# One ring for weights and modulation tiles, a new plan for the modulation sums, and a first norm fed by two channel tiles at a time

## The chip, the cores and the metric

The kernel runs on one core of a Trainium2 chip. The metric is the device time of one execution in microseconds (us). Before the change it is 1752.94 us, the median of three runs (1749.55 to 1754.62). The engines are TensorE (PE, with its weight loads as PEld), VectorE (DVE), ScalarE (ACT), GpSimd (POOL) and SyncE (SP), which here issues DMAs only.

## The reference, cut to what matters

Two layers with separate weights act on 384 tokens, 128 of a prompt and 256 of a sample, each with 1024 channels. Every layer is a half-step feed-forward block, a mixer (attention, a gating unit and a Fourier mix) and a second half-step feed-forward block. What the change touches is the modulation: nine vectors of 1024 per layer and per condition (prompt, sample), from a product of the condition with an own matrix of 4 MB for each.

```
m = (silu(cond) @ W['w_mod'][l] + W['b_mod'][l]).reshape(cond.shape[0], 1, N_MOD, D_MODEL)
z = _modulate(_rmsnorm(h, W['g_norm'][l, 0]), m[:, :, 0], m[:, :, 1])      # x * (1 + scale) + shift
h = h + 0.5 * m[:, :, 2] * _swiglu(z, w_gate, w_up, w_down)                # 1024 -> 2816 -> 1024
z = _modulate(_rmsnorm(h, W['g_norm'][l, 1]), m[:, :, 3], m[:, :, 4])
...mixer; h = h + m[:, :, 5] * mixed
z = _modulate(_rmsnorm(h, W['g_norm'][l, 2]), m[:, :, 6], m[:, :, 7])
h = h + 0.5 * m[:, :, 8] * _swiglu(z, w_gate, w_up, w_down)
```

## The kernel before, in words

Activations lie transposed, 128 channels by 384 tokens (hT, eight tiles; "channel tile k" is one of them). Each large matrix comes in pieces of 512 KB (`raw`, four row blocks of 128 by 256 columns, so runs of 1 KB in memory). ACT casts a piece to its high part (`whi`, L476), DVE subtracts to get the low part (`wlo`, L483), and TensorE forms three products per block: high with high (L500), high weights with low activations (L501), low weights with high activations (L502). A piece feeds 24 products of 384 columns. The parts have NB = 6 buffers, so splits run up to six pieces ahead of TensorE.

The program is a list of units, each one piece's products. After a unit come the split of the piece six further on (`ensure`), then what stands in `later`: evacuations, and one `mods.pop`. All engines run their streams in order; the order is the order in which the code is written. The four `raw` buffers are reused in turn, and SP waits for DVE to finish the piece four before.

Of the 18 modulation vectors (called segments (layer, index) here), 16 are summed on DVE by `ModPhase`: a segment's matrix comes in eight tiles of 512 KB (`mraw`, two buffers of their own, asked for by POOL, L168). For each tile there is one multiply-accumulate for each condition (`macc`, L178 for the first tile, L181 for the others), then four folds per segment (a transpose L192 into PSUM, a sum L193). Three units after the last fold, TensorE adds four small products (`msel`, L202) and DVE writes the result (`modt`, L204). `MOD_PLAN` says which segments are summed in which feed-forward block. Each `pop` issues as many steps as make the progress even over the units of the block. The first block has (0,2) to (0,7), the second five segments, the third five, the fourth and both mixers none.

Segments (0,0) and (0,1), scale and shift of the first norm, go another way, since the first block can't start without them. SP loads them in slices of 128 columns (`rawm`, runs of 512 B), two slices (one of each segment) for each channel tile; TensorE multiplies them (`modacc`, L245), ACT copies out (`accs`, L248), TensorE selects (L252), DVE adds the bias (L253). `start_z` then makes the normalised tile: ACT scales and shifts (L380) and rounds it to the high part (L381), DVE subtracts (L383). `start_joint` runs all eight channel tiles through the first six pieces into six PSUM banks, with the modulation of tile k+1 in between.

The names to follow: `start_joint`, `start_z`, `mod_load`, `mod_cols`, `fetch`, `split_hi`, `split_lo`, `ensure`, `ModPhase`, `ffn`, `mixer`, `prologue`.

Of the kernel before, what the change touches and what calls it, by code (L numbers as in the profile page):

```python
# [10 lines left out]
F32 = mybir.dt.float32  # L11
# [17 lines left out]
MB = 2  # L29
MOD_WAIT = 3  # L30
MOD_SLACK = 4
MOD_LAG = 3
MOD_PLAN = {
    (0, 0): [(0, s) for s in (2, 3, 4, 5, 6, 7)],
    (0, 1): [(0, 8)] + [(1, s) for s in (0, 1, 2, 3)],
    (1, 0): [(1, s) for s in (4, 5, 6, 7, 8)],
    (1, 1): [],
}
HOLD = 8
RAW_STATS = (5, 8)  # L40
START_POS = (1, 0, 0, 0, 0, 0, 0)
NX = NT + 2
NZ = 448
# [4 lines left out]
def kernel(  # L48
# [14 lines left out]
    rawp = ctx.enter_context(tc.tile_pool(name="rawp", bufs=4))  # L63
# [28 lines left out]
    prow = [tmp.tile([128, 128], F32, tag="t", name=f"prow{l}") for l in range(NL)]  # L92
# [41 lines left out]

    pending = []
# [9 lines left out]
    class ModPhase:  # L145
# [3 lines left out]
        def __init__(self, segs, n_units):  # L149
            self.segs, self.n_units = segs, max(1, n_units)  # L150
            self.loads = [(l, seg, k) for l, seg in segs for k in range(8)]
            self.raws = {}
            self.n_loaded = 0
            self.steps = deque()
            for l, seg in segs:
                for k in range(8):
                    for i in range(2):
                        self.steps.append(lambda l=l, seg=seg, k=k, i=i: self.mac(l, seg, k, i))
                for c_ in range(4):
                    self.steps.append(lambda l=l, seg=seg, c_=c_: self.fold(l, seg, c_))  # L160
            self.n_steps, self.emitted, self.unit = len(self.steps), 0, 0
            self.fins = deque()

        def load(self):
            if self.n_loaded < len(self.loads):
                l, seg, k = self.loads[self.n_loaded]
                raw = self.raws[l, seg, k] = self.pool.tile([128, 1024], F32, tag="mraw", name="mraw", bufs=MB)
                POOL.dma_start(out=raw, in_=w_mod[l][k * 128:(k + 1) * 128, seg * 1024:seg * 1024 + 1024])  # L168
                self.n_loaded += 1

        def mac(self, l, seg, k, i):
            if k == 0 and i == 0:
                self.acc = self.pool.tile([128, 2, 1024], F32, tag="macc", name="macc", bufs=1)
            while self.n_loaded < MB:
                self.load()
            raw = self.raws[l, seg, k]
            if k == 0:
                DVE.tensor_scalar(out=self.acc[:, i], in0=raw, scalar1=condT[:, 0, i:i + 1], scalar2=None,  # L178
                                  op0=ALU.mult)
            else:  # L180
                DVE.scalar_tensor_tensor(out=self.acc[:, i], in0=raw, scalar=condT[:, k, i:i + 1],  # L181
                                         in1=self.acc[:, i], op0=ALU.mult, op1=ALU.add)
            if i == 1:
                del self.raws[l, seg, k]
                self.load()
# [23 lines left out]
        def pop(self):  # L209
# [4 lines left out]
            due = min(self.n_steps, -(-self.n_steps * self.unit // self.n_units))  # L214
            while self.emitted < due:
                self.steps.popleft()()
                self.emitted += 1

        def need(self, *segs):
            while not all(x in mod_done for x in segs):  # L220
                if self.fins:
                    self.fins.popleft()[1]()
                else:
                    self.steps.popleft()()
                    self.emitted += 1
# [6 lines left out]
    def mod_load(l, seg, k):  # L232
        raw = st["startpool"].tile([128, 8, 128], F32, tag="st", name="rawm")
        c0 = seg * 1024 + k * 128
        SP.dma_start(out=raw, in_=w_mod[l][:, c0:c0 + 128].rearrange("(k p) m -> p k m", p=128))
        mod_raws[l, seg, k] = raw

    def mod_cols(l, seg, m):

        acc = ps_m.tile([128, 512], F32, tag="m", name="modacc")  # L240
        raws = [mod_raws.pop((l, seg + e, m)) for e in range(2)]
        for k in range(4):
            for j in range(4):
                kk = 4 * (j % 2) + k
                PE.matmul(acc[32 * j:32 * j + 32, 0:128], lhsT=condT[:, kk, :], rhs=raws[j // 2][:, kk, :],  # L245
                          start=(k == 0), stop=(k == 3))
        accs = st["startpool"].tile([128, 128], F32, tag="accs", name="accs", bufs=1)
        ACT.copy(accs, acc[:, 0:128])  # L248

        def fin():  # L250
            ps = abank("msel")
            PE.matmul(ps[:, 0:4], lhsT=accs, rhs=sel3, start=True, stop=True)  # L252
            DVE.tensor_tensor(out=modt[l][:, seg:seg + 2, m, :], in0=ps[:, 0:4].rearrange("p (e i) -> p e i", e=2),  # L253
                              in1=pcol[l][:, seg * 8 + m:seg * 8 + m + 9:8].unsqueeze(2).to_broadcast([128, 2, 2]),
                              op=ALU.add)
# [115 lines left out]
    def start_z(k, aside=lambda: None):  # L371
# [81 lines left out]
    def fetch(n):  # L453

        while nfetch[0] < n:
            it = items[nfetch[0]]
            k, n_ = it["shape"]
            raw = rawp.tile([128, 1024], F32, tag="raw", name="raw")
# [83 lines left out]
    def ffn(l, f, n, nxt, first=False):  # L542
        S = {}

        def open_pool():
            S["es"] = ExitStack()
            S["pool"] = mods.pool = S["es"].enter_context(tc.tile_pool(name="ffn", bufs=1))

        mods = ModPhase(MOD_PLAN[l, f], 44 - (6 if first else 2 + MOD_WAIT) + 18 - MOD_SLACK)

# [825 lines left out]
```

## Time and profile before

| quantity | us |
|---|---|
| median of three runs | 1752.94 |
| the profiled execution, its own time | 1752.7 |
| its span in the trace | 1750.9 |
| PE busy (share of the span) | 1703.3 (97%) |
| PEld, DVE, ACT, POOL busy | 1651.6, 1207.1, 716.6, 107.1 |

The profiled execution lasts 1.8 us longer than its span. A busy time of TensorE also holds pipelined overlap and stretches at a lower clock, so 97% does not say that only 3% could be saved. A product of 384 columns shows some 0.34 us in the trace, while products start every 0.17 us. A share over the whole span mixes the opening, three feed-forward blocks with modulation sums, one without, and two mixers; the stages have to be read one at a time.

### The profile page before, as it was taken

To read this page: it belongs to the slowest core of one execution; us is meant where nothing else is said; L and a number is where in the kernel's file an instruction comes from. 1 tells how busy PE (TensorE), PEld (TensorE's weight loads), DVE (VectorE), ACT (ScalarE), POOL (GpSimd) and SP (SyncE) were. 2 spreads that over 40 slices of the span, in tenths; PEclk is the share of its full clock that TensorE was granted. 3 is DMA by queue.
4 is the path that set the end of the run, shared out by engine and by line. 5 is a ranking of instruction groups with operands and counts; after the bars stand their busy time and mean duration, and the time that the engine had idled before them with its cause. 6 is when DMAs were issued, how large, how long until landed. Compare 5 with 4: busy or idle time off the path is not lost.

```text
span 1750.9 us, 25549 instructions
## 1 busy us (share of the span) xinstructions
PE 1703.3 (97%) x10081; PEld 1651.6 (94%) x10081; DVE 1207.1 (69%) x1789; ACT 716.6 (41%) x1217; POOL 107.1 (6%) x177
## 2 busy tenths in 40 slices
PE   7899998899999999999999999999999999999997
PEld 6899998888999999999999999998899999999997
DVE  4699999674564779898969899867456467534332
ACT  4423322363553463333345333236354446433331
POOL 0011110020000000000000000002000000000000
PEclk9999999999999999999999999999999999999999
DMA  9777666453333437776647677645433342544331
GB/s 289 234 217 216 216 202 205 143 168 117 109 97 109 133 123 238 218 225 207 187 151 218 213 230 221 202 143 171 117 112 97 109 126 84 164 122 132 118 124 37
DMA packets 236340, 286.36 MB, mean 164 GB/s; under 512 B 9725, under 2 KB 212974, under 8 KB 236220
## 3 DMA queue, kind: packets, MB, share of 16 engines
q1 hardware_dynamic: 215516, 211.03, 39.5%
q0 software_dynamic: 20704, 73.70, 13.9%
q8 instruction: 79, 1.29, 0.3%
q14 instruction: 41, 0.34, 0.1%
HBM read 282.07 MB, written 2.62 MB: 163 GB/s over the span
## 4 chain that ended last, share of the span: by engine, by line
PE 83%; issue 7%; DVE 4%; DMA 4%; SPq 1%; POOL 1%; ACT 0%; POOLq 0%; DVEq 0%; ACTq 0%
PE mm L500 24%; PE mm L502 23%; PE mm L501 23%; DMA mraw<-in_w_mod_dram 2%; DVE macc L181 2%; PE mm L507 1%; PE mm L509 1%; PE mm L508 1%; DMA rawm<-in_w_mod_dram 1%; DVE wlo L483 1%; PE mm L533 1%; PE mm L534 1%; PE mm L536 1%; PE raw L502 1%; PE raw L500 1%
## 5 line engine op out<-in xcount | busy, mean ns | idle before, releaser
L483 DVE TENSOR_TENSOR wlo<-raw,whi 128x1024 fp32r<-128x1024 f32 (+1 forms) x388 | 463.4, 1200 | 371.4 <-ACT whi L476 370.7
L476 ACT CAST whi<-raw 128x1024 fp32r<-128x1024 f32 (+1 forms) x388 | 397.2, 1031 | 558.7 <-PE mm L501 461.4
L500 PE MATMUL mm<-zh,whi 128*128 128x384 f32 x1784 | 608.5, 341 | 6.6 <-DVE hu L565 4.5
L502 PE MATMUL mm<-zh,wlo 128*128 128x384 f32 x1784 | 598.8, 336 | 0.4 <-DVE wlo L483 0.4
L501 PE MATMUL mm<-zl,whi 128*128 128x384 f32 x1784 | 598.5, 335 | 0.0
L500 PEld LDWEIGHTS mm<-zh,whi 128*128 128x128 f32 x1784 | 336.4, 189 | 14.5 <-DVE hu L565 5.6
L501 PEld LDWEIGHTS mm<-zl,whi 128*128 128x128 f32 x1784 | 336.6, 189 | 2.9 <-issue 1.7
L502 PEld LDWEIGHTS mm<-zh,wlo 128*128 128x128 f32 x1784 | 336.3, 189 | 0.7 <-DVE wlo L483 0.7
L181 DVE SCALAR_TENSOR_TENSOR macc<-mraw,condT,macc 128x1024 f32<-128x1024 f32 x224 | 280.6, 1281 | 39.8 <-DMA mraw<-in_w_mod_dram 39.7
L168 POOL DMA_DIRECT2D mraw<-in_w_mod_dram x128 | 68.7, 537 | 675.1 <-DVE macc L181 385.3
L560 ACT ACTIVATE ga<-mm 128x384 f32<-128x384 f32 x80 | 38.0, 489 | 78.0 <-PE mm L502 77.8
L404 DVE SCALAR_TENSOR_TENSOR h<-mm,gq,h 128x128 f32<-128x128 f32 x96 | 34.3, 411 | 39.5 <-PE mm L502 39.2
L565 DVE TENSOR_TENSOR hu<-ga,mm 128x384 f32<-128x384 f32 x88 | 45.5, 549 | 15.4 <-PE mm L502 14.0
L285 POOL TENSOR_TENSOR rstd<-var,mhalf 128x3 f32<-128x3 f32 x6 | 9.7, 1624 | 714.3 <-DVE var L283 714.3
L269 ACT ACTIVATE sq<-h 128x384 f32<-128x384 f32 x42 | 21.9, 522 | 71.2 <-DVE h L404 71.2
L192 DVE STREAM_TRANSPOSE mT<-macc 128x512 f32<-128x512 f32 x64 | 46.3, 723 | 0.8
L193 DVE TENSOR_REDUCE msum<-mT 128x16 f32<-128x512 f32 x64 | 44.3, 692 | 2.2
L1138 ACT ACTIVATE gth<-mm,hbg 128x384 f32<-128x384 f32 x48 | 27.2, 581 | 40.2 <-PE mm L502 40.2
L501 PE MATMUL mm<-tb,whi 128*128 128x384 f32 x128 | 43.0, 336 | 0.0
L507 PE MATMUL mm<-whi,zh 128*128 128x512 f32 x96 | 39.5, 411 | 0.0
L509 PE MATMUL mm<-whi,zl 128*128 128x512 f32 x96 | 37.5, 390 | 0.0
L508 PE MATMUL mm<-wlo,zh 128*128 128x512 f32 x96 | 37.4, 390 | 0.0
(469 smaller groups left out, 2662.8 us busy)
## 6 DMA issues: line engine op xcount, KB each, us to landing
mraw<-in_w_mod_dram POOLq DMA_DIRECT2D x128, 512.0 KB, 4.5
raw<-in_ffn_w_gate_dram SPq DMA_DIRECT2D x88, 512.0 KB, 4.5
raw<-in_ffn_w_up_dram SPq DMA_DIRECT2D x88, 512.0 KB, 4.4
raw<-in_w_in_dram SPq DMA_DIRECT2D x84, 512.0 KB, 3.8
raw<-in_ffn_w_down_dram SPq DMA_DIRECT2D x80, 512.0 KB, 3.7
rawm<-in_w_mod_dram SPq DMA_DIRECT2D x16, 512.0 KB, 7.3
raw<-in_w_out_dram SPq DMA_DIRECT2D x16, 512.0 KB, 3.4
raw<-in_ffn_w_down_dram SPq DMA_DIRECT2D x16, 256.0 KB, 3.1
```

The costliest lines, as they stand in the source:

```text
L168: POOL.dma_start(out=raw, in_=w_mod[l][k * 128:(k + 1) * 128, seg * 1024:seg * 1024 + 1024])
L181: DVE.scalar_tensor_tensor(out=self.acc[:, i], in0=raw, scalar=condT[:, k, i:i + 1], in1=self.acc[:, i], op0=ALU.mult, op1=ALU.add)
L192: DVE.transpose(out=ps, in_=self.acc[:, c_ // 2, (c_ % 2) * 512:(c_ % 2) * 512 + 512])
L476: ACT.copy(it["hi"], it["raw"])
L483: DVE.tensor_tensor(out=it["w"][1], in0=it["raw"], in1=it["hi"].bitcast(F32), op=ALU.subtract)
L500: PE.matmul(ps, lhsT=wh, rhs=xh, start=first, stop=False)
L501: PE.matmul(ps, lhsT=wh, rhs=xl, start=False, stop=False)
L502: PE.matmul(ps, lhsT=wl, rhs=xh, start=False, stop=last)
L507: PE.matmul(ps, lhsT=xh, rhs=wh, start=first, stop=False)
L508: PE.matmul(ps, lhsT=xh, rhs=wl, start=False, stop=False)
L509: PE.matmul(ps, lhsT=xl, rhs=wh, start=False, stop=last)
L565: DVE.tensor_tensor(out=u, in0=S.pop(("a", m)), in1=ps[:, 0:NT], op=ALU.mult)
```

## The change

- **One ring.** Weight pieces and modulation tiles share one ring of raw buffers (`raw_tile`): four anywhere, six inside a feed-forward block. A modulation tile is asked for by SP at its place in the program, no longer by POOL with two buffers of its own.
- **One plan.** A step is now a whole tile (two accumulates) or a fold. Steps are dealt out by the time that a table gives as free on DVE in each kind of unit (`DVE_FREE`), with a target at the gate (where the block's own gate is needed). The first block loses segment (0,7) to the mixer of layer 0; the second has four segments, the third five, the fourth one.
- **The opening.** `rawm` slices are 256 columns wide, for two channel tiles at a time (four pairs of slices, p = 0 to 3, in place of eight). Their order among the weights changes. The second parameter rows and two constants are loaded by POOL in the prologue, no longer by SP. Two groups of six products of the identity with itself stand on TensorE ahead of the first product. `start_z` makes the high part straight from the scale and shift on ACT, and DVE makes the full value itself.

```
-    (0, 0): [(0, s) for s in (2, 3, 4, 5, 6, 7)],
...
+    (0, 0): ([(0, 2), (0, 3), (0, 4)], [(0, 5), (0, 6)]),
+    (0, "m"): ([], [(0, 7)]),
+    (0, 1): ([(0, 8), (1, 0), (1, 1)], [(1, 2)]),
+    (1, 0): ([(1, 3), (1, 4)], [(1, 5), (1, 6), (1, 7)]),
+    (1, "m"): ([], []),
+    (1, 1): ([(1, 8)], []),
+DVE_FREE = {"half": 27, "up": 5, "mix": 10, "att": 3, "down": 27, "resid": 0}
...
+    def raw_tile():
+        n, more = raws["n"], raws["more"]
+        if n > 3 and not more:
+            n = 0
+        raws["n"] = n + 1 if n < (5 if more else 3) else 0
+        if n < 4:
+            return rawp.tile([128, 1024], F32, tag=f"raw{n}", name="raw")
+        return more.tile([128, 1024], F32, tag=f"raw{n}", name="raw")
...
+        def mac(self, l, seg, k):
+            if k == 0:
                 self.acc = self.pool.tile([128, 2, 1024], F32, tag="macc", name="macc", bufs=1)
...
+            raw = raw_tile()
+            SP.dma_start(out=raw, in_=w_mod[l][k * 128:(k + 1) * 128, seg * 1024:seg * 1024 + 1024])
+            for i in range(2):
+                if k == 0:
...
-            due = min(self.n_steps, -(-self.n_steps * self.unit // self.n_units))
-            while self.emitted < due:
-                self.steps.popleft()()
-                self.emitted += 1
+            u, g = self.unit, self.gate_at
+            all_, before, after = 20 * len(self.segs), sum(self.free[:g]), max(1, sum(self.free[g:]))
+            at_gate = max(20 * self.n_soon, all_ * before / (before + after))
+            if u <= g:
+                due = at_gate * sum(self.free[:u]) / before
+            else:
+                due = at_gate + (all_ - at_gate) * sum(self.free[g:u]) / after
+            while self.steps and self.emitted + self.weight[0] <= due + 1e-6:
+                self.step()
...
-        raw = st["startpool"].tile([128, 8, 128], F32, tag="st", name="rawm")
...
+        raw = st["startpool"].tile([128, 8, 256], F32, tag="st", name="rawm")
+        c0 = seg * 1024 + p * 256
+        SP.dma_start(out=raw, in_=w_mod[l][:, c0:c0 + 256].rearrange("(k p) m -> p k m", p=128))
...
-            ACT.activation(out=u[:, a:b], in_=t[:, a:b], func=AF.Identity, scale=s[:, i:i + 1], bias=sh[:, i:i + 1])
-        ACT.copy(hi[:, 0:NT], u)
-        aside()
+            ACT.activation(out=hi[:, a:b], in_=t[:, a:b], func=AF.Identity, scale=s[:, i:i + 1], bias=sh[:, i:i + 1])
+        for (a, b, i) in RG:
+            DVE.tensor_scalar(out=u[:, a:b], in0=t[:, a:b], scalar1=s[:, i:i + 1], scalar2=sh[:, i:i + 1],
+                              op0=ALU.mult, op1=ALU.add)
...
+                        PE.matmul(pss[5][:, 0:128], lhsT=ident, rhs=ident, start=True, stop=True)
...
+                busy(START_BUSY[0])
+                split_hi(ids[0])
+                split_lo(ids[0])
                 fin[0] = mod_cols(l, 3 * n, 0)
-                split_hi(ids[0])
+                split_hi(ids[1])
                 fin[0]()
-                start_z(0, lambda: split_lo(ids[0]))
...
+                busy(START_BUSY[1])
+                start_z(0)
+                split_lo(ids[1])
...
+                        if (k, it) in START_MOD:
+                            p = START_MOD[k, it]
+                            fin[p] = mod_cols(l, 3 * n, p)
...
-                            prow_load(1, SP)
...
+        prow_load(1, POOL)
```

The order of the instructions shows what moved. First ACT's stream in the opening, from the last copy of the input (`h`) on: `rbs` is the row of norm factors, `accs` the modulation result, `whi` a weight piece's high part, `zh` the first product's activations. Before:

```order
L1276 COPY h_116<-xT 128x384
L322 COPY rbs<-rb 128x384
L248 COPY accs<-modacc 128x128
L476 CAST whi<-raw 128x1024
L380 ACTIVATE zu<-zt,modt_100 128x128
L380 ACTIVATE zu<-zt,modt_100 128x256
L381 CAST zh_263<-zu 128x384
```

The same place on ACT of the changed program:

```order
L1316 COPY h_116<-xT 128x384
L341 COPY rbs<-rb 128x384
L496 CAST whi<-raw 128x1024
L264 COPY accs<-modacc 128x256
L496 CAST whi<-raw 128x1024
L399 ACTIVATE zh_280<-zt,modt_100 128x128
L399 ACTIVATE zh_280<-zt,modt_100 128x256
```

Two casts of weight pieces now stand ahead of the first `zh`, one of them ahead of `accs`, and the rounding behind it is gone. Next SP's stream of DMAs behind the input's; `rawm` are the first norm's weights, `raw` weight pieces, `prow` the second layer's parameter rows, with two constants behind them before the next piece. Before:

```order
L235 DMA rawm<-in_w_mod_dram 128x8x128 x2
L461 DMA raw<-in_ffn_w_gate_dram 128x4x256
L235 DMA rawm<-in_w_mod_dram 128x8x128 x2
L461 DMA raw<-in_ffn_w_up_dram 128x4x256
L461 DMA raw<-in_ffn_w_gate_dram 128x4x256
L235 DMA rawm<-in_w_mod_dram 128x8x128 x4
L461 DMA raw<-in_ffn_w_gate_dram 128x4x256
L235 DMA rawm<-in_w_mod_dram 128x8x128 x2
L461 DMA raw<-in_ffn_w_up_dram 128x4x256
L461 DMA raw<-in_ffn_w_gate_dram 128x4x256
L235 DMA rawm<-in_w_mod_dram 128x8x128 x6
L106 DMA prow_95<-in_b_mod_dram 72x128
```

SP in the changed program, from the same place on:

```order
L251 DMA rawm<-in_w_mod_dram 128x8x256 x2
L481 DMA raw<-in_ffn_w_gate_dram 128x4x256
L481 DMA raw<-in_ffn_w_up_dram 128x4x256
L481 DMA raw<-in_ffn_w_gate_dram 128x4x256
L251 DMA rawm<-in_w_mod_dram 128x8x256 x4
L481 DMA raw<-in_ffn_w_gate_dram 128x4x256
L481 DMA raw<-in_ffn_w_up_dram 128x4x256
L481 DMA raw<-in_ffn_w_gate_dram 128x4x256
L251 DMA rawm<-in_w_mod_dram 128x8x256 x2
L481 DMA raw<-in_ffn_w_up_dram 128x4x256 x2
```

The pieces follow the last `rawm` at once, and each slice is twice as large. Last, DVE in the first feed-forward block around a segment's folds, between two evacuations of the up product (`hu`); `macc` is the modulation sum, `mT` and `msum` the fold. Before:

```order
L483 TENSOR_TENSOR wlo_1383<-raw_1379,whi_1381 128x1024
L181 SCALAR_TENSOR_TENSOR macc_1101<-mraw_1312,condT_99,macc_1101 128x1024
L192 STREAM_TRANSPOSE mT_1389<-macc_1101 128x512
L193 TENSOR_REDUCE msum_1388<-mT_1389 128x16
L483 TENSOR_TENSOR wlo_1422<-raw_1418,whi_1420 128x1024
L192 STREAM_TRANSPOSE mT_1424<-macc_1101 128x512
L193 TENSOR_REDUCE msum_1388<-mT_1424 128x16
L192 STREAM_TRANSPOSE mT_1427<-macc_1101 128x512
L193 TENSOR_REDUCE msum_1388<-mT_1427 128x16
L192 STREAM_TRANSPOSE mT_1430<-macc_1101 128x512
L193 TENSOR_REDUCE msum_1388<-mT_1430 128x16
L565 TENSOR_TENSOR hu_1457<-ga_1375,mm_1392 128x384
```

The second segment's folds in the changed program:

```order
L195 SCALAR_TENSOR_TENSOR macc_1157<-raw_1546,condT_99,macc_1157 128x1024 x2
L203 STREAM_TRANSPOSE mT_1551<-macc_1157 128x512
L204 TENSOR_REDUCE msum_1550<-mT_1551 128x16
L503 TENSOR_TENSOR wlo_1586<-raw_1582,whi_1584 128x1024
L203 STREAM_TRANSPOSE mT_1588<-macc_1157 128x512
L204 TENSOR_REDUCE msum_1550<-mT_1588 128x16
L203 STREAM_TRANSPOSE mT_1591<-macc_1157 128x512
L204 TENSOR_REDUCE msum_1550<-mT_1591 128x16
L503 TENSOR_TENSOR wlo_1624<-raw_1620,whi_1622 128x1024
L203 STREAM_TRANSPOSE mT_1626<-macc_1157 128x512
L204 TENSOR_REDUCE msum_1550<-mT_1626 128x16
L192 TENSOR_SCALAR macc_1629<-raw_1630,condT_99 128x1024 x2
```

Before, three folds stand between the last weight piece and the evacuation that TensorE's bank waits for; now one fold stands there, with the next segment's first two accumulates, and no more than two folds follow one another.

## Rows read from the trace of the kernel before

**Rows 1.** The page's first line

```profile
span 1750.9 us, 25549 instructions
```

**Rows 2.** Stages by window: first feed-forward block, mixer's start, third block

```profile
core 0: us, PE busy (x) PEld busy (x) DVE busy (x) ACT busy (x) POOL busy (x), PEclk, DMA share, GB/s
65.40:344.00 278.60, 260.02 (x1492) 257.00 (x1491) 245.12 (x297) 87.53 (x130) 24.74 (x46) 0.97 0.66 205
344.00:462.00 118.00, 117.55 (x635) 104.92 (x634) 73.50 (x151) 60.83 (x119) 14.48 (x18) 1.00 0.46 135
906.00:1184.00 278.00, 277.56 (x1630) 275.55 (x1630) 241.95 (x314) 108.38 (x167) 24.76 (x43) 1.00 0.65 201
```

**Rows 3.** What TensorE waited for, 75 to 350 us: total, times, longest

```profile
PE msel L202 <- DVE msum L193: 8.7, 3, 5.0
PE msel L202 <- DVE gq L707: 5.3, 1, 5.3
PE mm L500 <- DVE hu L565: 4.5, 3, 2.6
```

**Rows 4.** VectorE by line, 65.4 to 344 us: busy, mean ns | idle before

```profile
L181 DVE SCALAR_TENSOR_TENSOR macc<-mraw,condT,macc 128x1024 f32<-128x1024 f32 x84 | 105.0, 1281 | 17.5 <-DMA mraw<-in_w_mod_dram 17.4
...
L192 DVE STREAM_TRANSPOSE mT<-macc 128x512 f32<-128x512 f32 x24 | 17.4, 723 | 0.3
L193 DVE TENSOR_REDUCE msum<-mT 128x16 f32<-128x512 f32 x24 | 16.6, 692 | 0.8
...
L178 DVE TENSOR_SCALAR macc<-mraw,condT 128x1024 f32<-128x1024 f32 x12 | 8.6, 747 | 0.0
```

**Rows 5.** A window behind one of these waits

```profile
150.00:155.00 5.00, 2.68 (x17) 2.57 (x18) 4.93 (x9) 2.44 (x5) 0.00 (x0) 0.81 0.29 97
```

**Rows 6.** TensorE's timeline: first product of the block, first behind it

```profile
65.44 0.33 PE L500 MATMUL mm<-zh,whi 128*128 128x384 f32 x1
...
343.98 0.34 PE L500 MATMUL raw<-xh,whi 128*128 128x386 f32 x1
```

**Rows 7.** The chain of waits: third block's norm and the next norm

```profile
906.42 1.81 POOL rstd L285
1185.45 1.83 POOL rstd L285
```

**Rows 8.** The opening by window

```profile
2.00:8.00 6.00, 2.38 (x11) 2.30 (x12) 0.42 (x3) 2.06 (x5) 1.56 (x4) 1.00 0.85 286
17.00:20.00 3.00, 3.00 (x26) 2.34 (x29) 0.11 (x1) 0.85 (x1) 0.00 (x0) 0.50 1.11 343
20.00:25.00 5.00, 3.64 (x34) 2.48 (x26) 3.49 (x5) 2.62 (x6) 0.00 (x0) 1.00 1.21 293
50.00:53.00 3.00, 0.05 (x1) 0.05 (x1) 0.23 (x1) 1.21 (x2) 0.00 (x0) 0.62 1.09 371
```

**Rows 9.** The chain of waits in the opening, 42 to 52 us

```profile
42.36 1.71 SPq L106
...
47.34 4.32 DMA raw<-in_ffn_w_up_dram
```

**Rows 10.** The opening's timeline, TensorE and ACT: start, duration, idle before

```profile
15.00 0.98 ACT L380 ACTIVATE zu<-zt,modt 128x128 f32<-128x128 f32 x2
16.57 0.68 PE L500 MATMUL mm<-zh,whi 128*128 128x384 f32 x1 [2.07 <-ACT zh L381]
25.38 1.08 PE L245 MATMUL modacc<-rawm,condT 128*32 128x128 f32 x32 [0.72 <-DMA rawm<-in_w_mod_dram]
52.95 0.59 PE L252 MATMUL msel<-sel,accs 128*128 128x4 f32 x2 [5.30 <-ACT accs L248]
```

**Rows 11.** The page's costliest groups: splits of weight pieces

```profile
L483 DVE TENSOR_TENSOR wlo<-raw,whi 128x1024 fp32r<-128x1024 f32 (+1 forms) x388 | 463.4, 1200 | 371.4 <-ACT whi L476 370.7
L476 ACT CAST whi<-raw 128x1024 fp32r<-128x1024 f32 (+1 forms) x388 | 397.2, 1031 | 558.7 <-PE mm L501 461.4
```

**Rows 12.** Tile mraw: asked for to landed

```profile
DMA to landing us min/median/max: 3.7/4.5/6.8
```

More of the change, by code (lines that the diff above doesn't have):

```diff
@@ L91 @@
     mhalf = const.tile([128, 4], F32, name="mhalf")
-    prow = [tmp.tile([128, 128], F32, tag="t", name=f"prow{l}") for l in range(NL)]
+    prow = [tmp.tile([128, 128], F32, tag="t", name="prow0"),
+            tmp.tile([128, 128], F32, tag="ws", name="prow1", bufs=1)]
     pcol = [const.tile([128, 128], F32, name=f"pcol{l}") for l in range(NL)]
@@ L145, with __init__ @@
     class ModPhase:
[L149 to L153, printed above, removed]
+        def __init__(self, soon, late):
+            self.segs, self.n_soon, self.free, self.gate_at = soon + late, len(soon), [], 0
+            segs = self.segs
             self.steps = deque()
@@ L156, in __init__ @@
                 for k in range(8):
-                    for i in range(2):
-                        self.steps.append(lambda l=l, seg=seg, k=k, i=i: self.mac(l, seg, k, i))
+                    self.steps.append(lambda l=l, seg=seg, k=k: self.mac(l, seg, k))
                 for c_ in range(4):
                     self.steps.append(lambda l=l, seg=seg, c_=c_: self.fold(l, seg, c_))
-            self.n_steps, self.emitted, self.unit = len(self.steps), 0, 0
+            self.weight = deque(([2] * 8 + [1] * 4) * len(segs))
@@ L162, in __init__ @@
+            self.emitted, self.unit = 0, 0
             self.fins = deque()
[L164 to L172, printed above, removed]
-                self.acc = self.pool.tile([128, 2, 1024], F32, tag="macc", name="macc", bufs=1)
[L174 to L185, printed above, removed]
@@ L223, in need @@
                 else:
-                    self.steps.popleft()()
-                    self.emitted += 1
+                    self.step()
         def close(self):
@@ L457, in fetch @@
             k, n_ = it["shape"]
-            raw = rawp.tile([128, 1024], F32, tag="raw", name="raw")
+            raw = raw_tile()
             v = it["raw"] = raw[:, 0:k * n_].rearrange("p (k n) -> p k n", k=k)
@@ L546, in open_pool @@
             S["es"] = ExitStack()
-            S["pool"] = mods.pool = S["es"].enter_context(tc.tile_pool(name="ffn", bufs=1))
-        mods = ModPhase(MOD_PLAN[l, f], 44 - (6 if first else 2 + MOD_WAIT) + 18 - MOD_SLACK)
+            S["pool"] = mods.pool = raws["more"] = S["es"].enter_context(tc.tile_pool(name="ffn", bufs=1))
+        mods = ModPhase(*MOD_PLAN[l, f])
         def pop():
@@ L593, in run, with busy @@
+                def busy(n):
+                    for _ in range(n):
+                        PE.matmul(pss[5][:, 0:128], lhsT=ident, rhs=ident, start=True, stop=True)
                 fin = {}
-                fetch(1)
+                fetch(3)
                 loads(1)
-                fetch(3)
-                loads(2, 3)
+                loads(2)
                 fetch(4)
-                loads(4)
                 start_t(0)
+                start_t(1)
+                busy(START_BUSY[0])
+                split_hi(ids[0])
@@ L685, in ffn @@
             fill = first or i >= ids[n_first] + MOD_WAIT
+            if fill:
+                mods.free.append(DVE_FREE["up" if ty == "u" and kh == 1 else "half"])
             add_unit(piece(i, kh, (ty, mp), evs_(ev_g if ty == "g" else ev_u, mp), fill), [i])
@@ L698, in run @@
                         resid(2 * mp + e, ps, S["gate"], nxt)
-                if mp < 3:
+                if mp * 6 + kb < 24 - MOD_SLACK:
                     pop()
+            if mp * 6 + kb < 24 - MOD_SLACK and not (mp == 3 and nxt is None):
+                mods.free.append(DVE_FREE["resid" if kb == 5 else "down"])
             return run
@@ L738, in end @@
             mods.close()
+            raws["more"] = None
             S["es"].close()
@@ L1258, in prologue @@
         prow_load(0, POOL)
+        prow_load(1, POOL)
+        for dst, src in ((win, k_win), (rev, k_rev)):
+            POOL.dma_start(out=dst, in_=src)
         cond_setup()
```

138 lines of the change are left out of this document (74 added, 64 removed).

## The prediction

> **What bounds the kernel now.** The span is 1750.9 us [rows 1]. I first cut it into stages by window, since a mean over the span hides where TensorE stands still. In the third feed-forward block, 906 to 1184 us, TensorE is busy 277.56 of 278.00 us: it is the bound, and nothing on another engine can give time there. VectorE is busy 241.95 us of it, 87%, and that with five segments of modulation sums [rows 2]. The mixer's start is as full. The first feed-forward block is different: 260.02 of 278.60 us, at a mean granted clock of 0.97, with VectorE at 245.12 us. Then I read what TensorE waited for in that block: 8.7 and 5.3 us for fold results at `msel` and 4.5 us for `hu`, in sum 18.5 us, all of them VectorE [rows 3]. Each is VectorE late with its queue, since it works its stream in order. Behind such a wait the granted clock is 0.81 over five us [rows 5], so a wait costs more than its own length. By line, the six segments hold VectorE for 105.0 + 17.4 + 16.6 + 8.6 = 147.6 us, 24.6 each, and it stands idle another 17.4 us for their tiles [rows 4].
>
> How much this block loses is read off against the third. From one norm to the next there, 1185.45 - 906.42 = 279.0 us, lie 44 pieces of gate and up and 24 of down, four of these half size: 44 x 24 + 20 x 24 + 4 x 12 = 1584 products, 0.1762 us each with all that comes along [rows 7]. The first block, without its opening, has 38 such pieces and the same 24: 1440 products, 253.7 us. It takes 343.98 - 65.44 = 278.5 us [rows 6]. So 24.8 us are lost.
>
> The third place is the opening, up to 65.44 us. Its windows show the DMA queues full: their share stands above 1 (1.21 from 20 to 25 us, 1.09 from 50 to 53), as it counts packets that overlap [rows 8]. The rate depends on what is moved: 293 GB/s where mostly `rawm` with runs of 512 B is under way, 343 in a mixture, 371 where weight pieces with runs of 1 KB are alone. Then the chain shows SP at 42.36 us still sending parameter rows; the next weight piece is asked for at 47.34 and lands 4.32 us later [rows 9]. ACT waits for that piece with the next `accs` behind it, and TensorE stands still for 5.30 us [rows 10].
>
> **The opening, step by step.** From 2 to 8 us, 6.0 x 286 GB/s = 1.72 MB arrive, the input and the small rows [rows 8]. Up to the last `rawm` there follow 8.39 MB of `rawm`, six pieces (3.15 MB) and the 0.16 MB which POOL now asks for: 11.7 MB. With `rawm` in runs of 1 KB I take the mean of 343 and 371, 357 GB/s: 32.8 us, so the last slice lands at 40.8. The ends are 371 (39.5 us) and 293 (47.9); the value lies by the former since the weight pieces are the row nearest in run length.
>
> The Trainium skill, "DMA: Bandwidth & Descriptors", section Specifications, has 512 B as the least transfer for line rate, so by that rule runs of 1 KB bring nothing over 512 B. The rows disagree, 293 against 371. By the rule the last slice would land at 47.9, which is a rival below.
>
> TensorE's own path to the same place: the first product has moved back. On ACT two casts stand ahead of the first `zh`, one of them ahead of `accs`, and the first pair of slices is twice as large. The first piece lands behind 2.1 + 0.16 + 0.52 MB, at 8.0 + 7.8 = 15.8; its cast takes 1.03 [rows 11], `accs` some 0.4, the second cast 1.03, the scaled copy 0.98 [rows 10]: 19.3 us, where today the first product starts at 16.57. What stands behind these casts on ACT is `accs` and so `msel`, TensorE's start. The shorter chain saves the rounding, but its place was not what ended the wait. Then VectorE needs 0.56 for the low activations (an estimate, a third of a 1.20 us split and overhead) and two low parts of 1.20 [rows 11], and a third of channel tile 0 (6 products, 1.06) follows: 23.3. Four channel tiles of 18 products are 12.7 us, two `modacc` of twice 1.08 us [rows 10] 4.3: 40.3. So slices and TensorE arrive together, and I take 40.8. Behind it come the last `modacc` with 2.2 us, one selection of 0.59 [rows 10] and three channel tiles, 54 x 0.176 = 9.5: the block proper starts at 53.1, against 65.44: a gain of 12.3 us. The seventh piece follows the last slice on SP, lands some 1.5 us behind it and isn't needed until 53, so the 5.30 us wait goes and nothing late takes its place. The ends: 12.8 (TensorE's path alone) and 5.2 (293 GB/s).
>
> The twelve identity products lie in the wait ahead of the first product, today 2.07 us, now 2.7 longer. Taken at the 0.34 us of three times as many columns [rows 6] they would fill 4.1 of these 4.8 us. After its wait TensorE ran at a granted clock of 0.50 from 17 to 20 us, its lower level of 1.2 GHz [rows 8]. If the products keep 2.4 GHz, 1 to 2 us are won in channel tile 0, but the low parts of pieces two and three end that stage. I count zero.
>
> **The first block.** It loses segment (0,7). VectorE has 245.1 - 24.6 = 220.5 us of work left in 254 us, 87%: the share at which the third block shows no wait. The steps no longer come evenly: the order has one tile (2.5 us) in most units, where a unit takes 24 x 0.176 = 4.2 us and its piece 1.2, and one fold with two first accumulates, 1.4 + 1.5 us, ahead of the `hu` that had three folds ahead of it. A unit with two folds costs 1.2 + 2.8 = 4.0. So no unit exceeds 4.2 by itself, and the cushion of six split pieces stays whole. The ring removes waits for tiles as well: a tile is asked for when VectorE leaves the one six before, five tiles ahead. With 40 tiles and 62 pieces in 62 units that is 5 / 1.65 x 4.2 = 12.8 us of notice against 4.5 us to landing, 6.8 at most [rows 12]. SP's queue now holds these waits, and the pieces queued behind them are wanted in that same order. I take 253.7 and 1 us left over: 254.7, a gain of 23.8. Ends: 24.8, and 12.4 if half of the loss stays.
>
> **The other stages.** Mixer 0 gets segment (0,7): at most 73.5 + 24.6 = 98.1 us of VectorE in 118 us [rows 2], 83%. The nearest row, the third block with 87%, loses 0.44; I take 0.5 us. The far end is the first block of today, 24.8 lost in 278.6 at 88%: 10.5 us in 118. The second and third blocks lose nothing to VectorE today, so neither the ring nor one segment fewer brings anything there; the fourth gets one segment where the third carries five: nothing.
>
> **Sum.** 12.3 + 23.8 - 0.5 = 35.6 us; span 1750.9 - 35.6 = 1715.3. The profiled execution takes 1752.7 us, 1.8 more than its span and 0.2 less than the median of 1752.94. Predicted: 1717 us.
>
> **Rivals.**
> - *Bytes bound the opening.* If the rate stays at 293 GB/s, the gain is 5.2 there: 35.6 - 7.1 = 28.5, so 1724 us. For it: the queues are full throughout. Against: 371 with runs of 1 KB.
> - *VectorE's lag stays in part.* Half the loss remains in the first block, and mixer 0 pays 5 us, as the work is moved and not removed: 12.3 + 12.4 - 5 = 19.7, so 1733 us. For it: two accumulates now never part, so the queue comes in larger lumps. Against: the third block.
> - *Slower: the shared ring starves the weights.* Place: the three blocks with sums, 102, 100 and 108 tiles, 52 turns of the ring. If a landing exceeds 12.8 us, each turn is late by the excess, and the pieces stand in the same line. Six split pieces hide 25 us in each block. It outweighs the 35.6 us from (35.6 + 76) / 52 = 2.1 us of excess, a landing of 15 us; at 16 us it costs 166 - 76 = 90, so 1717 + 90 = 1807 us. Against: 4.5 us median. For it: SP's one queue now carries all.
> - *It doesn't do what it says.* The opening stays bound by bytes with its slow start, and the waits for `hu` and `msel` come back with the order: within 5 us of 1753.
>
> **Chances.** Forecast 0.72, bytes 0.13, lag 0.09, ring 0.03, no effect 0.03. A difference under 0.3%, 5.3 us, can't be told from none here. Faster 0.94, same 0.03, slower 0.03. The range: at the upper end the lag's 1733; at the lower end the terms' best, 12.8 + 24.8 = 37.6 or 1715, less the 3.4 us by which the fastest run lies under the median: 1711.
>
> **What would show it.** The block's first product near 53 us and the mixer's first near 308; the last `modacc` at 41 to 43 with DMA rates near 350 up to there; the first product near 19; no wait of TensorE for `msum`, `gq` or `hu` above 1 us; VectorE near 87% in the first block; no TensorE wait in mixer 0. A late `modacc` with rates under 300 would show the bytes; waits at `msel` the lag; ACT waiting for `raw` in the second and third blocks the ring.

## The result and the profile after

The changed kernel takes 1720.31 us, the median of four runs (1719.27 to 1721.3), and the kernel before 1752.49 beside it: a ratio of 0.9817, 95% interval 0.98 to 0.9834. Forecast were 1717, range 1711 to 1733. The time lies in the range, in part by luck: of the two large terms one was 3 us too large and the other 3 us too small, and the experiments found a cause for the second that the prediction does not name.

The profiled execution has this first line on its page; it answers to [rows 1]:

```profile
span 1717.6 us, 25319 instructions
```

The stages by window, with the columns of [rows 2]: most of the first feed-forward block, the start of mixer 0, and the third block.

```profile
56.00:308.00 252.00, 252.00 (x1486) 250.55 (x1484) 222.34 (x273) 90.87 (x131) 0.00 (x0) 1.00 0.71 213
308.00:426.00 118.00, 116.86 (x635) 103.83 (x629) 92.31 (x171) 60.41 (x119) 14.54 (x18) 1.00 0.58 175
...
871.00:1150.00 279.00, 278.79 (x1638) 276.42 (x1637) 242.91 (x315) 110.25 (x169) 2.31 (x3) 1.00 0.68 206
```

In the first block TensorE now stands still for nothing and its clock is 1.00, against 260.02 of 278.60 us and 0.97 in [rows 2]. VectorE's share of the block is 88% (222.34 of 252.00), just as it was before (245.12 of 278.60). Mixer 0 has taken over sums of the segment that left (92.31 us of VectorE against 73.50) and TensorE loses 1.14 us there, where it lost 0.45.

What TensorE waited for over the whole program: total, times, longest. The three rows of [rows 3] are gone, none of them has a successor.

```profile
PE modacc L261 <- DMA rawm<-in_w_mod_dram: 2.5, 2, 1.6
PE rb L338 <- POOL rstd L304: 2.2, 4, 0.9
...
PE mm L520 <- ACT A L892: 0.7, 1, 0.7
```

VectorE's accumulates on the page, busy and mean ns, then idle before them: the 17.4 us that they waited for tiles in the first block [rows 4] are 0.0 over all blocks.

```profile
L195 DVE SCALAR_TENSOR_TENSOR macc<-raw,condT,macc 128x1024 f32<-128x1024 f32 x224 | 277.2, 1280 | 0.0
```

TensorE's timeline, start and duration: the block's first product and the first one of the mixer behind it, as in [rows 6].

```profile
56.36 0.33 PE L520 MATMUL mm<-zh,whi 128*128 128x384 f32 x1
...
307.98 0.44 PE L520 MATMUL raw<-xh,whi 128*128 128x386 f32 x1
```

The norm behind the block is on POOL's timeline at 312.29, before at 348.16. From the block's first product to that norm, which is the stretch compared below, it was 348.16 - 65.44 = 282.72 us, and now it is 312.29 - 56.36 = 255.93:

```profile
312.29 1.80 POOL L304 TENSOR_TENSOR rstd<-var,mhalf 128x3 f32<-128x3 f32 x1 [2.38 <-DVE var L302]
```

So the opening gave 65.44 - 56.36 = 9.1 us and the first block 26.8. From norm to norm mixer 0 went from 279.34 to 280.73, so 1.4 lost. The other four stages gave 0.3, -0.4, 0.0 and -0.7. In sum it is 33.8 us up to the last norm, and 33.3 in the span.

The opening by window, as in [rows 8]. The last number is GB/s: nearly constant from 12 to 46 us. The last slice is asked for at 32.0 us and lands 11.7 later, at 43.7.

```profile
8.00:12.00 4.00, 3.14 (x19) 2.90 (x17) 1.59 (x5) 3.45 (x7) 0.87 (x1) 1.00 1.04 331
...
16.00:20.00 4.00, 3.02 (x41) 2.21 (x42) 1.34 (x3) 2.27 (x3) 0.00 (x0) 1.00 1.10 348
20.00:25.00 5.00, 4.78 (x28) 4.00 (x26) 4.51 (x8) 2.82 (x6) 0.00 (x0) 1.00 1.09 347
...
40.00:46.00 6.00, 6.00 (x55) 5.23 (x57) 4.66 (x8) 2.29 (x4) 0.00 (x0) 1.00 1.09 348
46.00:53.00 7.00, 7.00 (x51) 6.59 (x43) 4.37 (x9) 5.04 (x8) 0.00 (x0) 1.00 0.30 97
```

TensorE's timeline in the opening (the rest of its rows are the products in between), start, duration, and the idle time before with what ended it:

```profile
16.15 1.93 PE L261 MATMUL modacc<-rawm,condT 128*32 128x256 f32 x32 [1.59 <-DMA rawm<-in_w_mod_dram]
18.92 0.61 PE L269 MATMUL msel<-sel,accs 128*128 128x4 f32 x4 [0.83 <-ACT accs L264]
19.38 1.58 PE L609 MATMUL raw<-ident 128*128 128x128 f32 x12
...
27.23 1.93 PE L261 MATMUL modacc<-rawm,condT 128*32 128x256 f32 x32 [0.93 <-DMA rawm<-in_w_mod_dram]
30.25 0.50 PE L269 MATMUL msel<-sel,accs 128*128 128x4 f32 x4
34.75 1.93 PE L261 MATMUL modacc<-rawm,condT 128*32 128x256 f32 x32
...
44.56 1.93 PE L261 MATMUL modacc<-rawm,condT 128*32 128x256 f32 x32
```

The first product stands at 21.04. The second pair of slices is still waited for (0.93), the third and fourth are not: from 27.23 on TensorE itself sets the time. The 5.30 us wait of [rows 10] is gone.

### The profile page after: what moved, and what is told of

The parts are those of the page before. It is cut to its first block, busy times and chain, and to the rows that moved or that the text cites. A ratio compares the mean times of both kernels' runs of the same rounds, so it can differ in the third digit from the quotient of the medians.

```text
span 1717.6 us, 25319 instructions
## 1 busy us (share of the span) xinstructions
PE 1693.6 (99%) x9977; PEld 1642.2 (96%) x9977; DVE 1212.7 (71%) x1801; ACT 712.6 (41%) x1205; POOL 40.8 (2%) x55
## 4 chain that ended last, share of the span: by engine, by line
PE 94%; ACT 2%; DMA 1%; DVE 1%; SPq 1%; issue 1%; POOL 1%; POOLq 0%; DVEq 0%; ACTq 0%
PE mm L520 28%; PE mm L522 28%; PE mm L521 28%; PE mm L527 1%; PE mm L528 1%; PE mm L529 1%; ACT zu L370 1%; DMA rawm<-in_w_mod_dram 1%; PE pv L1072 1%; PE pT L119 1%; PE S L1027 1%; PE mm L553 1%; PE mm L556 0%; PE mm L554 0%; POOL rstd L304 0%
## 5 line engine op out<-in xcount | busy, mean ns | idle before, releaser
L195 DVE SCALAR_TENSOR_TENSOR macc<-raw,condT,macc 128x1024 f32<-128x1024 f32 x224 | 277.2, 1280 | 0.0
L370 ACT ACTIVATE zu<-zt,modt,sg 128x128 f32<-128x128 f32 (+1 forms) x60 | 29.6, 541 | 16.3 <-DVE zt L357 16.3
L1044 ACT ACTIVATE sc<-sc,nm 128x384 f32<-128x384 f32 x32 | 19.5, 609 | 37.9 <-DVE nm L1041 37.8
## 6 DMA issues: line engine op xcount, KB each, us to landing
rawm<-in_w_mod_dram SPq DMA_DIRECT2D x8, 1024.0 KB, 11.7
```

## The experiments

Totals of single runs can be compared to a few us only (the kernel before took 1755.45, 1756.81 and 1750.93 us beside the three groups), so the kernels are compared by the first block's length in the trace, from its first product to the norm behind it. Where five segments are in it that length is 255.93 to 255.94 us in all seven kernels, so 0.1 us can be told apart where TensorE doesn't wait. A block with waits may vary more: each kernel has one trace, and the totals of the kernel before range from 1749.55 to 1756.81 us, so differences against it hold to a few us. The expectations speak of the block up to the mixer's first product, which is 251.6 for the changed kernel; that is 4.3 us shorter.

| kernel | segments | deal | tiles | last step in unit | block begins | block, us |
|---|---|---|---|---|---|---|
| before | 6 | even | own | 52 | 65.44 | 282.72 |
| e14_before_long | 6 | even | own | 59 | 64.79 | 265.66 |
| e12_short_stretch | 6 | even | own | 52 | 56.48 | 275.05 |
| e7_opening_alone | 6 | even | own | 59 | 56.26 | 260.39 |
| e8_six_even | 6 | even | ring | 59 | 56.48 | 260.04 |
| e1_six_segments | 6 | table | ring | 59 | 57.97 | 260.39 |
| e10_six_own | 6 | table | own | 59 | 56.27 | 270.68 |
| e2_own_buffers | 5 | table | own | 59 | 56.35 | 255.93 |
| after | 5 | table | ring | 59 | 56.36 | 255.93 |

The deal is even or by the table, and the tiles have two buffers of their own or the shared ring. The first theories were that the segment that left (A), the ring (B) or the deal (C) made the gain. One part was put back at a time.

**e1_six_segments**, 1723.61 us.

```
-    (0, 0): ([(0, 2), (0, 3), (0, 4)], [(0, 5), (0, 6)]),
-    (0, "m"): ([], [(0, 7)]),
+    (0, 0): ([(0, 2), (0, 3), (0, 4)], [(0, 5), (0, 6), (0, 7)]),
+    (0, "m"): ([], []),
```

> The changed kernel with segment (0,7) put back into the first feed-forward block (six segments there, none in mixer 0); ring, deal and opening stay. VectorE then has 222.0 + 24.6 = 246.6 us of work in that block, of which TensorE alone needs 251.6. Theory A (the segment that left is the larger part of the gain): VectorE falls behind at 98%, TensorE waits for products of its folds or for hu, and the block grows from 251.6 to about 262 us (256 to 270); mixer 0 goes back from 280.7 to 279.3; total about 1729. Theory B (the ring did it, by ending the 17.4 us in which VectorE stood waiting for tiles) and theory C (the deal did it): the block stays within 2 us of 251.6 and the total is 1719 to 1721.

The block grew by 4.5 us to 260.39 and mixer 0 went back to 279.34. Up to the mixer's first product it was 254.5: A missed its 262, B and C their 2 us. With the rest of the change in place the segment's move is worth 4.5 - 1.4 = 3.1 us, not 26.8.

**e2_own_buffers**, 1717.78 us.

```
+            if self.own:
+                while self.n_loaded < 2:
+                    self.load()          # POOL.dma_start into mraw, bufs=2
+                raw = self.raws.pop((l, seg, k))
...
-            S["pool"] = mods.pool = raws["more"] = S["es"].enter_context(tc.tile_pool(name="ffn", bufs=1))
+            S["pool"] = mods.pool = S["es"].enter_context(tc.tile_pool(name="ffn", bufs=1))
+            mods.own = True
```

> The changed kernel, but inside the feed-forward blocks the modulation tiles have two buffers of their own again, asked for through POOL with the same look-ahead as before the change, and the weights a ring of four; five segments, deal and opening stay. Theory A (load): VectorE waits for tiles some 10 us again but has 30 us to spare; the first block stays within 3 us of 251.6, total 1719 to 1724. Theory B (ring): most of the gain is lost, the first block takes 265 us or more and the total is above 1733. Theory C (deal) says as A.

255.93 us, as with the ring. VectorE doesn't wait for tiles there at all, where some 10 us were expected. B falls: with five segments the ring is worth nothing.

**e3_even_deal**, 1743.77 us.

```
-DVE_FREE = {"half": 27, "up": 5, "mix": 10, "att": 3, "down": 27, "resid": 0}
+DVE_FREE = {"half": 1, "up": 1, "mix": 1, "att": 1, "down": 1, "resid": 1}
...
-            at_gate = max(20 * self.n_soon, all_ * before / (before + after))
+            at_gate = all_ * before / (before + after)
```

> The changed kernel with all steps dealt evenly over the units (the table of free times set to one value, no target at the gate but the even one); ring, segments and opening stay. Theories A (load) and B (ring): the first block stays within 2 us of 251.6, mixer 0 within 1 us of 280.7, total 1719 to 1723. Theory C (the deal keeps the folds out of the units in which hu or the resid falls): waits of TensorE at msel or hu come back, the first block takes 260 us or more, and the blocks with four and five segments lose as well, total above 1730.

The first block stayed at 255.94, so C falls for it as well. But the second took 288.07 and the fourth 290.77 us (278.6 each in the changed kernel), by one wait each ahead of the gate, 6.7 and 10.6 us:

```profile
PE msel L213 <- DVE msum L204: 17.3, 2, 10.6
```

The edit held two things, the table and the target at the gate. **e11_flat_table**, 1720.53 us, is the first line of it alone.

> The changed kernel with the table of free times flat but the target at the gate kept. The even deal without the target cost 24 us, by waits of 6.7 and 10.6 us at msel ahead of the gate in the second and fourth block, while the first block took 251.6 us as before. If it was the target, all blocks are within 1.5 us of the changed kernel's and the total is 1718 to 1723; if it was the table, the second and fourth block again take 288 and 290 us and the total is above 1735.

Second and fourth block are back at 278.59 and 278.64: the target does it, and the plan with one segment in the fourth block can't do without. The table is worth 2.2 us in mixer 0 (282.91 without it against 280.73 us), and costs 0.4 us in the third block (279.03 against 279.38) and 0.8 in mixer 1 (278.54 against 279.34).

No part alone carried the gain, so all but the opening was put back. **e7_opening_alone**, 1721.75 us (the plan of before as lists in the old order; flat table; own buffers as in e2).

```
-    (0, 0): ([(0, 2), (0, 3), (0, 4)], [(0, 5), (0, 6)]),
...
+    (0, 0): ([], [(0, s) for s in (2, 3, 4, 5, 6, 7)]),
...
+DVE_FREE = {"half": 1, "up": 1, "mix": 1, "att": 1, "down": 1, "resid": 1}
```

> The new opening with all else put back: six, five, five and no segments by the old list in the four feed-forward blocks, none in mixer 0, steps dealt evenly with no target, two buffers of their own asked for through POOL (a step is still a whole tile). Putting back one part at a time cost the first block nothing (own buffers), nothing (even deal) and 2.9 us (sixth segment). If the 26.9 us are these three together, the block takes 276 to 280 us again and the total is 1743 to 1746. If part of it came with the opening (a block that starts without a debt, at full clock), the block takes 255 to 270 us and the total is 1722 to 1736.

260.39 us (254.5 up to the mixer, just under the expected range): with the old plan, the even deal and the old buffers the block still loses only 4.5 us. Something else had come with the code. VectorE's share is no guide here: it is busy 243.11 of 254.40 us, 96%, and TensorE waits for it once, 2.4 us.

```profile
56.30:310.70 254.40, 251.98 (x1490) 250.21 (x1488) 243.11 (x294) 90.38 (x129) 24.52 (x47) 1.00 0.73 225
```

**e8_six_even**, 1721.76 us (e1 with the flat table).

> Six segments in the first block and the table of free times flat, with the ring. Theory B' (the sixth segment hurts only where VectorE also waits for tiles, which the ring ends): the first block takes 254 to 258 us, as with six segments and the deal (254.5), total 1723 to 1727. Theory C' (it hurts only where the deal also puts steps into the units with hu and folds): the block takes 265 us or more, total above 1733.

**e10_six_own**, 1731.9 us (e1 with own buffers).

> Six segments in the first block and the modulation tiles' own two buffers through POOL, with the new deal. Theory B' (ring): VectorE waits for tiles again, some 15 us, and at 98% has nowhere to take them from: the first block takes 265 us or more, total above 1731. Theory C' (deal): the block takes 254 to 258 us, total 1721 to 1725.

e8 gives 260.04, e10 270.68 (254.2 and 264.5 up to the mixer, the latter half a us short of the 265 of theory B'). So with six segments the new deal needs the ring: in e10 VectorE waits for tiles again in the block, and TensorE pays 10.3 us. With the even deal the ring isn't needed: e7, with the same two buffers, waits 0.7 us for tiles.

```profile
DVE macc L209 <- DMA mraw<-in_w_mod_dram: 15.8, 11, 2.3
```

What e7 shares with the changed kernel, apart from the opening and steps of whole tiles, is the number of units that get steps. Before, the steps end at unit 44 - 6 + 18 - 4 = 52 of the block's 62; now every unit with 6 mp + kb < 21 gets some, 38 + 21 = 59. So the progress of the kernel before was even over 52 units and not over the whole block. Its windows up to VectorE's last fold, which is in unit 52 and ends at 317.4 us, and behind it (columns as above) show what I had averaged away:

```profile
65.00:317.40 252.40, 233.87 (x1341) 230.88 (x1339) 232.10 (x276) 80.46 (x116) 24.74 (x46) 0.97 0.68 210
317.40:344.00 26.60, 26.55 (x153) 26.52 (x154) 13.42 (x23) 7.30 (x14) 0.00 (x0) 0.94 0.51 159
```

and the waits of VectorE in the first of the two:

```profile
DVE macc L181 <- DMA mraw<-in_w_mod_dram: 17.4, 16, 2.3
DVE wlo L483 <- ACT whi L476: 1.6, 1, 1.6
DVE hu L565 <- ACT ga L560: 0.6, 1, 0.6
```

232.10 + 17.4 + 1.6 + 0.6 = 251.7 of 252.4 us: full for 52 units, then busy for 50%. Two kernels test that.

**e14_before_long**, 1734.96 us: the kernel before, 59 in place of 52.

```
-        mods = ModPhase(MOD_PLAN[l, f], 44 - (6 if first else 2 + MOD_WAIT) + 18 - MOD_SLACK)
+        mods = ModPhase(MOD_PLAN[l, f], 44 - (6 if first else 2 + MOD_WAIT) + 21)
...
-                if mp < 3:
+                if mp * 6 + kb < 21:
                     pop()
```

> The kernel before with one number changed: the modulation steps of a feed-forward block are spread over 59 units in place of 52 (of 62 in the first block). All else is as before, the old opening, six segments, single accumulates, own buffers through POOL. Theory S (the stretch: 147.6 us of sums in 52 units are 2.84 us a unit, with 97.5 / 62 = 1.57 us of other work 4.41 us of VectorE where TensorE takes 4.16; in 59 units they are 4.07): the first block takes 254 to 260 us in place of 278.5, total 1728 to 1735. Theory O (the block starts late out of the old opening, or single accumulates wait for tiles): it takes 270 us or more, total above 1744.

**e12_short_stretch**, 1735.7 us: e7 with the last step in unit 52 again.

```
-                mods.free.append(DVE_FREE["resid" if kb == 5 else "down"])
+                mods.free.append(1 if mp * 6 + kb < 14 else 0)
```

> The new opening alone (six segments, even deal, own buffers; 254.5 us in the first block), with the steps of a block ended by unit 52 in place of 59. Theory S (stretch): the first block takes 268 to 280 us, total 1735 to 1747. Theory O (it was the opening or the whole-tile steps): the block stays at 254 to 258 us, total 1721 to 1725.

e14's block takes 265.66 us (258.6 up to the mixer, within the 254 to 260 of theory S), e12's 275.05 (270.9, within 268 to 280). So spreading the steps over seven more units alone gives 282.72 - 265.66 = 17.1 us in the old kernel, and taking it back costs 14.7 in the kernel with the new opening (e7). In e12 TensorE's waits for fold results and `hu` are back:

```profile
PE msel L229 <- DVE msum L220: 10.4, 4, 3.6
...
PE mm L536 <- DVE hu L602: 2.1, 4, 0.7
```

Two runs are on the opening. **e4_short_runs**, 1722.27 us.

```
-        SP.dma_start(out=raw, in_=w_mod[l][:, c0:c0 + 256].rearrange("(k p) m -> p k m", p=128))
+        for h in range(2):
+            SP.dma_start(out=raw[:, :, 128 * h:128 * h + 128],
+                         in_=w_mod[l][:, c0 + 128 * h:c0 + 128 * h + 128].rearrange("(k p) m -> p k m", p=128))
```

> The changed kernel with each rawm slice of 256 columns asked for as two transfers of 128 columns each, so runs of 512 B in place of 1 KB, the same bytes in the same order to the same places. Theory D (the length of the runs sets the rate): from 12 to 46 us the rate falls from 348 to about 293 GB/s, the last slice lands about 6 us later, and the first block begins at 61 to 63 us in place of 56.4; total about 1726. Rival (it was not the run but the order and the smaller number of tiles): the rate stays above 340 and the block begins within 1 us of 56.4.

Its windows:

```profile
12.00:16.00 4.00, 2.54 (x19) 2.38 (x19) 2.79 (x8) 0.88 (x2) 0.02 (x1) 1.00 1.20 292
16.00:20.00 4.00, 2.05 (x32) 1.59 (x32) 0.28 (x1) 1.32 (x2) 0.00 (x0) 1.00 1.11 346
...
30.00:35.00 5.00, 5.00 (x41) 4.15 (x34) 0.35 (x2) 0.56 (x2) 0.00 (x0) 0.70 1.21 292
```

From 8 us on the rate falls to 291 to 297 in six of the nine windows and stays at 339 to 346 in two: the length of the runs sets the rate, as D said. (The transfers are also half as large, 512 KB, but weight pieces of that size moved at 371 in [rows 8].) The price is smaller than D's 6 us: the block begins at 60.27, 3.9 later than in the changed kernel. Of that 2.1 are the second pair's later landing (its products start at 29.30 for 27.23) and 1.7 a drop of the clock behind it (below; they take 3.67 us for 1.93). The third and fourth pair are not waited for.

**e5_no_identity**, 1720.82 us.

```
-START_BUSY = (6, 6)
+START_BUSY = (0, 0)
```

> The changed kernel without its twelve identity products. If they keep the granted clock up, TensorE falls to half of it behind the wait for the first slice, as it did before the change (0.50 from 17 to 20 us), the first pair's 32 modacc products take about 3.5 in place of 1.93 us, the first channel tile about 3 us longer, and the first block begins 1 to 3 us later than 56.4; total 1719 to 1724. If they do nothing, the clock and the beginning stay, total 1718 to 1721.

```profile
16.36 3.57 PE L261 MATMUL modacc<-rawm,condT 128*32 128x256 f32 x32 [3.38 <-DMA rawm<-in_w_mod_dram]
```

The clock is 0.57 from 16 to 20 us, the first pair's products take 3.57 in place of 1.93 us, and the block begins at 57.82. The identity products are worth up to 1.5 us, where I had counted zero.

**e13_busy_p1**, median 1717.43 us of four runs (1717.02 to 1718.78), a ratio of 0.9807 to the kernel before beside it, 95% interval 0.9791 to 0.9824.

```
+        for _ in range(n_busy):
+            PE.matmul(acc[:, 0:128], lhsT=ident, rhs=ident, start=True, stop=True)
...
+                            fin[p] = mod_cols(l, 3 * n, p, 8 if p == 1 else 0)
...
                 loads(3)
+                prow_load(1, SP)
```

> The changed kernel with eight more identity products ahead of the second pair's modacc, in its own bank (that wait is 0.9 to 1.6 us long, and in two of eight executions the granted clock fell to 0.75 behind it, where the 32 products took 3.4 to 3.5 us in place of 1.93), and with the second parameter rows and two constants asked for by SP behind the last slice, no longer by POOL ahead of the input. If the clock holds and 0.16 MB less stand ahead of the second pair (0.45 us at 348 GB/s), the first block begins at 55.8 to 56.4 in every execution, total 1717 to 1719. If the second pair's landing isn't set by the bytes ahead of it, or the clock falls all the same, it begins at 56.4 to 58 and the total is 1719 to 1721.

```profile
24.74 1.95 PE L258 MATMUL modacc<-ident 128*128 128x128 f32 x16
26.62 1.93 PE L263 MATMUL modacc<-rawm,condT 128*32 128x256 f32 x32
```

The second pair is no longer waited for and the block begins at 55.75 us, a little earlier than expected and 0.6 ahead of the changed kernel's. All four runs lie below all four of the changed kernel, but they come from another group and the intervals overlap, so by the totals it is not shown to be faster than the changed kernel. Which of its two edits does it is open.

## Why the prediction was right, and where not

**The first block: the size nearly right, the reason incomplete.** The weak step is "VectorE has 245.1 - 24.6 = 220.5 us of work left in 254 us, 87%: the share at which the third block shows no wait". I took VectorE's share over the whole block as the cause of the loss and one segment less as the cure. The share doesn't tell: it is 88% before, with 18.5 us of waits, 88% after, with none, and 96% in e7, with 2.4. What the prediction left out is that the rewrite also deals the steps out over 59 units in place of 52. The old due rule, whose removed line (`n_steps * unit // n_units`) stands in the diff, gives it: 147.6 us of sums [rows 4] in 52 units are 2.84 us a unit, with 97.5 / 62 = 1.57 us of other work 4.41, where a unit of TensorE takes 24 x 0.1747 = 4.19 us. In 59 units they are 4.07. The third block fits as well: its five segments lie in 44 - 5 + 18 - 4 = 53 of 68 units, 123.0 / 53 + 119.0 / 68 = 4.07 us, and it shows no wait. Behind unit 52 VectorE had time to spare, but TensorE had already waited. (That no more than two folds follow one another does not hold for the block's last segment: three stand in a row from 301.27 to 305.70 us. TensorE waits for none of them.)

The parts, each a step from one kernel to the next: the stretch 17.1 us (before to e14), the new opening and steps of whole tiles 5.3 more (e14 to e7; the two were not taken apart), and the sixth segment 4.5 (e7 or e1 to the changed kernel). As steps of one chain they add up to the 26.8 in any case; the pair of e12 and e7 gives 14.7 for the stretch, so it depends on the rest. What the segment is worth without the stretch no run shows. By the same division five segments in 52 units are 123.0 / 52 + 1.57 = 3.94 us, below 4.19 (an estimate), so the predicted cure might have removed most of the loss by itself. Shown is that the stretch gives some 17 us with all six segments in place, and that behind it the segment's move is worth 4.5 us less the 1.4 of mixer 0.

The term came out 3 us short since its bound was too high: 0.1762 us per product were read from norm to norm [rows 7] and hold the norm's own 2 us. The block takes 251.62 / 1440 = 0.1747. The 1 us left over for waits was not needed. The mixer's first product stands at 307.98, near the forecast 308, only because a block that began 3.3 us late was 3.1 us shorter than forecast.

**The ring.** VectorE's waits for tiles went from 17.4 us to 0, but that the ring ended them is not shown: e2 without it has none and e7 0.7 us, while e14, with the steps of single accumulates, still has 13.2. Nor was the ring worth time in the first block with five segments (e2). It pays only beside six segments and the new deal (e10 against e1, 10.3 us). The rival in which the ring starves the weights did not come: on the page 512 KB pieces and tiles take 3.4 to 4.3 us from issue to landing, in the median of each kind.

**Mixer 0** cost 1.4 us for an expected 0.5, inside its bounds.

**The opening** was the mis-sized term, 9.1 us for 12.3. The rate was as forecast, 348 for 357 GB/s, and the rival of the bytes fell with it; e4 shows that the run length is the cause. By the Trainium skill, "DMA: Bandwidth & Descriptors", section Specifications, 512 B suffice for line rate; the measured 291 to 297 against 348 GB/s decide against it here. What failed is the path to the fourth pair, on TensorE predicted at 40.3 and taken as 40.8, where the slices were to arrive: TensorE came to it at 44.56. The first product came 1.7 us late (21.04 for 19.3), as the first piece's cast could start only at 17.55 and not at 15.8; the second pair was waited for, 0.93 us; and the selections of the second and third pair, 0.50 each, were not in the sum. That is 3.7 of the 4.3 us. The last slice was late too, 43.7 for 40.8, but not waited for. I had checked only whether the last slice is late, and it was the second that stopped TensorE.

## What to carry over

Read the share of an in-order engine over the stretch in which its side work is dealt out, not over the stage: work per unit against the unit's length on the bound engine tells in one division whether it falls behind, and spreading the same work over more units gave some 17 us here without removing any of it. When a change has several parts, read also the constants that move along with the rewrite. Two parts that relieve the same engine need not add: before one of them gets the credit, or loses it, a run is needed with that part alone. For a chain of transfers check each arrival against the consumer's path, the early ones first.

## What the runs showed of the hardware

Behind a wait of some 1.5 us for the second pair the granted clock fell in some executions and not in others, with the same instructions around it. e1 and e2 differ only in what comes after the opening. TensorE's timeline of e1, at a clock of 0.74 from 25 to 30 us:

```profile
27.20 3.50 PE L261 MATMUL modacc<-rawm,condT 128*32 128x256 f32 x32 [1.52 <-DMA rawm<-in_w_mod_dram]
```

The same row of e2: the wait is 1.60 us long and the clock 1.00.

```profile
27.21 1.93 PE L277 MATMUL modacc<-rawm,condT 128*32 128x256 f32 x32 [1.60 <-DMA rawm<-in_w_mod_dram]
```

The block then begins at 57.97 in place of 56.35 us. The Trainium skill, "TensorE: Matmul & The Clock Gate", Part 1, says that the same kernel shows a different number of products at the low clock from run to run. These rows, of two kernels that are alike up to there, fit that. e3 and e4 show the drop too (waits of 1.60 and 1.89 us, products of 3.42 and 3.67); e8 and e11 don't (1.64 and 1.47 us, products of 1.93). The changed kernel's four runs lie at 1719.3 and 1721.3; that the same 1.6 us separates them is likely but not shown, since only one of them has a trace here.

Transfers of 1 MB with several others under way took 11.7 us from issue to landing (median of eight). Bytes over rate placed landings too early in the prediction, the first piece's by some 1.7 us and the last slice's by 2.9. Of that 0.4 and 1.0 us come from the rate, which was 331 GB/s from 8 to 12 us and 348 behind in place of 357 (an estimate from these rows); the rest is open.
